# One chain for the head groups, the short convolution of blocks 2 and 3 inside the delta-rule groups, and w3's low parts on VectorE

## The chip, the cores and the metric

The kernel runs on one core of a Trainium2 chip. Its engines work at the same time and wait for each other by semaphores: TensorE (PE for matmuls, PEld for the weight loads beside them), VectorE (DVE), ScalarE (ACT), GpSimd (POOL) and SyncE (SP), which here issues every DMA. Each engine takes its own instructions in the order in which they stand in the program. The metric is device microseconds of one execution, lower is better: the median of some runs. A profile is one further execution, taken by the hardware profiler.

## What is computed

One layer of a streaming encoder for 2048 prompt tokens and 32 sample tokens with their own states, D = 1024. All heads read one normalised input through one projection; their outputs are joined by W_out, and a SwiGLU block and a gated input embedding follow:

```python
hn = rmsnorm(h, W['norm_mix'][i])
proj = hn @ W['w_in'][i]
qkv_pre, z, ba, u5, cc = jnp.split(proj, [OFF_Z, OFF_BA, OFF_S5, OFF_CC], axis=-1)
ya, s_gdn, b_gconv = gdn_mixer(qkv_pre, z, ba, ...)   # conv of width 4 + silu on q, k, v, then the delta rule
yb, s_s5 = s5_mixer(u5, ...)                          # 16 groups x 64 complex states, then gelu and a GLU
yc, b_conv = conformer_conv(cc, ...)                  # GLU, causal depthwise conv of width 31, LayerNorm, swish
h = h + jnp.concatenate([ya, yb, yc], axis=-1) @ W['w_out'][i]
hf = rmsnorm(h, W['norm_ffn'][i])
h = h + (jax.nn.silu(hf @ W['ffn_w1'][i]) * (hf @ W['ffn_w3'][i])) @ W['ffn_w2'][i]
h = h + (p[i] @ W['pe_w'][i]) * jax.nn.sigmoid(h @ W['pe_gate_w'][i])
y = rmsnorm(h, W['norm_final'])
```

The outputs are y, and the new states of the delta rule, of both convolutions and of S5, for prompt and sample. The delta rule carries its state from chunk to chunk, so its blocks run one after the other; S5 and the two convolutions need only the projections of their block and what a block hands to the next.

## The kernel before

**Tiling.** Features lie on partitions, tokens along the row. The tokens make four blocks of 512; the last one has the 32 sample tokens too (544, done as two halves of 272). Phase A runs over the blocks 0 to 3 (called A0 to A3 here) and makes the projections; phase F runs over the same blocks (F0 to F3): w_out, the hidden layer with w1 and w3, w2, then pe and gate, then the final norm.

**Dense matmuls.** An fp32 operand is split in a high and a low part, and each product is made of three passes: high weight by high input, low by high, high by low (`dense`, `_dense`, L120: 8 input tiles by 3 passes is a group of 24 matmuls). `load_weight` (L81 to L104) loads a weight by DMA (`wr`), ScalarE copies the high part (L94, `wh`), and the low part `wl` is subtracted by GpSimd the first time (L96), stored in DRAM (`lo_`), and loaded from there by the later blocks. So subtractions of phase F's weights happen in F0 alone. Weights have three buffers each; `dense` writes into three PSUM buffers (`ps_d`), which VectorE empties.

**Phase A** (`PhaseA.block`): for each block the squares and norm, `u5` (L657), the gate and value of the conformer's GLU (`ccg`, `cca`, L707 to L712, stored as `xcd`), then twelve short convolutions (`PhaseA.conv`: the projection goes to `raw`, L607, then one scaled copy and three fused multiply-adds into `gacc`, L612 to L614, tanh and one more step, L617, stored as `sild`), then four `z` (L730 to L733, stored as `zgd`).

**Heads.** Everything else of the mixers is in generators: `conf` (62 multiply-adds `cacc` on VectorE a block, L813, then transposes, statistics L827, `cxn` L846 to L851, stored to `mixT` at L852), `gdn_group` (half a block of 256 tokens, and one for the sample tokens; triangular solve, transpose `XT` L961, state `S`, `zy` L1079, stored to `mixT` at L1080), `s5_unit` (two blocks at once; `X` L498, `ps_y` L518, `gq` L537, `ps_glu` L547) and, once, `s5_init` (the S5 constants; `ps_kg` L352). `dense` calls `G.step`, and each time enough matmul columns have gone by, every running chain of generators emits its next piece and says with `yield k` for how many further steps it pauses. This sets the order in which the program is written; a scheduler then sets the order on each engine, by the ranks `first`, `heads` and `later` and by its own model of times.

**Order before.** After A0, `s5_init` is emitted whole, at rank `heads`. During A1 to A3 one chain runs conformer block 0 and delta-rule block 0, and from A2 a second one runs S5 unit 0. Both are flushed at the end of phase A. In F0 to F2 a chain runs the conformer and delta-rule block of the next block, in F0 S5 unit 1 behind them, and each chain is flushed at the end of its block:

```python
for b in range(NB):
    nb = b + 1
    if nb < NB:
        G.start(run(conf_of(nb), gdn_of(nb), *(s5_of(u) for u in range(1, G.NU) if max(u * G.UB - 2, 0) == b)))
    pf.block(b)
    G.flush()
```

**Queue.** `PhaseF.block` begins with loads of `mixT` into `hb` (L1124), which need all heads of its block, splits them in `fah` (ScalarE) and `fal` (L1105, VectorE or GpSimd) for w_out, and adds the input (L1126). It ends with the final norm (L1222) and eight stores `out_yT` (L1223). All of these DMAs stand in one queue, SP's, in the order of the program, with the loads of weights between them.

Of the kernel before, what the change touches and what calls it, by code (L numbers as in the profile page):

```python
# [8 lines left out]
F32 = mybir.dt.float32  # L9
# [7 lines left out]
P = 128  # L17
# [63 lines left out]
def load_weight(G, src, K, name, key):  # L81


    nc = G.nc
    shp = [P] + (list(K) if isinstance(K, tuple) else [K]) + [P]
    with G.first():
        wr = G.wraw.tile(shp, F32, tag="wr", name=f"wr_{name}")
        nc.sync.dma_start(wr, src)
        wh = G.whi.tile(shp, F32R, tag="wh", name=f"wh_{name}")
        wl = G.wlo.tile(shp, F32R, tag="wl", name=f"wl_{name}")  # L90
        kept = G.low.get((name, key))
        if kept is not None:
            nc.sync.dma_start(wl.bitcast(F32), kept)
        nc.scalar.activation(wh, wr, AF.Copy)  # L94
        if kept is None:
            nc.gpsimd.tensor_tensor(wl, wr, wh.bitcast(F32), op=ALU.subtract)  # L96
            if G.NB > 1:
                kept = G.dd.tile(shp, F32, tag=f"lo_{name}{key}", name=f"lo_{name}{key}")
                G.low[(name, key)] = kept
                nc.sync.dma_start(kept, wl.bitcast(F32))  # L100
    return wh, wl
# [105 lines left out]
def s5_init(G, A, tp, pspool):  # L207
# [78 lines left out]
    for m in (1, 2, 4):  # L286
# [128 lines left out]
def s5_unit(G, A, u, wp, pspool):  # L415
# [14 lines left out]
    for jq in range(4):  # L430
# [17 lines left out]

        yield 2

# [54 lines left out]

        yield 2

# [29 lines left out]
        V.scalar_tensor_tensor(gq[:, jh], t, 1.0, yf, op0=ALU.add, op1=ALU.mult)  # L537
        yield 2
    spc = 512 // NCT
# [23 lines left out]
class PhaseA:  # L563


    def __init__(self, G, A, ctx):
# [13 lines left out]
        self.gm = const("gmix", [P, KD], A.norm_mix)  # L580
        self.cw = const("cw", [P, 12, 4], A.conv_w)
        V.tensor_scalar(self.cw, self.cw, 0.5, None, op0=ALU.mult)
        wr = G.wraw.tile([P, KD, 8], F32, tag="wr", name="wr_ba")
# [8 lines left out]
    def conv(self, m, jj, b, hf, hl, bc, n, last, t0):  # L592
# [16 lines left out]
        if last:  # L609
            nc.gpsimd.tensor_copy(taild[:, m], raw[:, W:W + 3])  # L610
        acc = wp.tile([P, W], F32, tag="gacc", name="gacc")
        nc.scalar.activation(acc, raw[:, 0:W], AF.Copy, scale=cw[:, m, 0:1])  # L612
# [9 lines left out]
    def block(self, b):  # L622
# [76 lines left out]
        for j in range(2):  # L699
# [13 lines left out]
            if not last:  # L713
                nc.sync.dma_start(G.xcd[b + 1][:, j, 0:30], xc[:, BLK - 30:BLK])
        with G.later():
            for g in gs:
                for _ in g:
                    pass
        for h in range(NH):
            self.conv(4 + h, 2 * h, b, hf, hl_, bc, n, last, t0)  # L720
            self.conv(h, 2 * h + 1, b, hf, hl_, bc, n, last, t0)
        for h in range(NH):
            self.conv(8 + h, 8 + h, b, hf, hl_, bc, n, last, t0)
        for h in range(NH):
            w = load_weight(G, A.w_in[12 + h], KD, "z", h)
            zz = wp.tile([P, n], F32, tag="gacc", name="zz")
            for c0, cn in chunks_of(n):
                cs = slice(c0, c0 + cn)
                p_ = dense(G, G.psD, "pd", w, hf, hl_, ks, c0, cn)
                V.tensor_tensor(zz[:, cs], p_[:, :cn], bc[:, cs], op=ALU.mult)  # L730
            th = wp.tile([P, n], F32, tag="gth", name="zth", bufs=1)
            nc.scalar.activation(th, zz, AF.Tanh, scale=0.5)
            V.scalar_tensor_tensor(zz, th, 1.0, zz, op0=ALU.add, op1=ALU.mult)  # L733
            nc.sync.dma_start(G.zgd[b][:, h], zz)
# [120 lines left out]
def gdn_group(G, A, sp, pspool, T, tw, nt, nw, S, b, c_out):  # L855
# [8 lines left out]
    kq = sp.tile([P, 8, nn], F32, tag="kq", name="kq", bufs=1)  # L864
    nc.sync.dma_start(kq, G.sild[b][:, 0:8, c_out:c_out + nn])
    vf = sp.tile([P, NH, nn], F32, tag="vf", name="vf", bufs=1)
    nc.sync.dma_start(vf, G.sild[b][:, 8:12, c_out:c_out + nn])
    yield 2
# [92 lines left out]
    V.transpose(XT.rearrange("p w c -> p (w c)"), X.rearrange("p w c -> p (w c)"))  # L961
    yield 3

# [263 lines left out]
def trunk_kernel(ctx: ExitStack, tc: tile.TileContext, A):  # L1227
# [56 lines left out]
    G.mixT = [dd.tile([P, KD, n], F32, tag=f"mixT{b}", name=f"mixT{b}") for b, n in enumerate(G.ns)]  # L1284
    G.sild = [dd.tile([P, 12, n], F32, tag=f"sild{b}", name=f"sild{b}") for b, n in enumerate(G.ns)]
    G.zgd = [dd.tile([P, NH, n], F32, tag=f"zgd{b}", name=f"zgd{b}") for b, n in enumerate(G.ns)]
# [23 lines left out]
    with G.heads():  # L1310
# [55 lines left out]
    def run(*gens):  # L1366

        for g in gens:
            yield from g

    with ExitStack() as cx:
        pa = PhaseA(G, A, cx)
        pa.block(0)
        with R("s5i") as tp, G.heads():
            s5_init(G, A, tp, G.psM)

        with R("s5_0") as w5:
            G.start(run(conf_of(0), gdn_of(0)))
            for b in range(1, NB):
                if b == G.UB:  # L1380
                    G.start(s5_unit(G, A, 0, w5, G.psM))
                pa.block(b)
            if NB == G.UB:
                G.start(s5_unit(G, A, 0, w5, G.psM))
            G.flush()
    pf = PhaseF(G, A, ctx)
    for b in range(NB):
        nb = b + 1
        if nb < NB:

            G.start(run(conf_of(nb), gdn_of(nb), *(s5_of(u) for u in range(1, G.NU) if max(u * G.UB - 2, 0) == b)))
        pf.block(b)
        G.flush()

# [114 lines left out]
```

## Time and profile before

| what | value |
|---|---|
| median of three runs | 2914.17 us (2912.3 to 2915.87) |
| the profiled execution | 2906.6 us |
| its span in the trace | 2904.8 us |
| mean granted TensorE clock | 0.976 |
| busy: PE, DVE, ACT, POOL | 2775.6, 1769.2, 931.4, 625.4 us |
| stages, by the first matmul of each: A1, A2, A3 | 189.5, 336.8, 521.3 us |
| F0, F1, F2, F3 | 706.9, 1291.5, 1835.5, 2367.5 us |

The trace's span is 1.8 us shorter than its execution's time. The busy time of an engine counts its instructions from start to end; a busy PE at a clock under 1 does less. A row of the waits names the instruction that waited, `<-`, and the one that released it, then the total, how many times and the longest. A row of the timeline has a start, a duration, engine, line, operation, `out<-in`, shape and count; in brackets is the idle time before it.

### The profile page before, as it was taken

How to read it: one execution, taken by the hardware profiler on the slowest of the kernel's cores; microseconds unless marked ns; L12 is line 12 of the kernel's file. 1: busy time of each engine (PE TensorE's matmuls, PEld its weight loads, DVE VectorE, ACT ScalarE, POOL GpSimd, SP SyncE). 2: the span in 40 equal slices, each digit the busy share in tenths (PEclk: the TensorE clock that was granted, in tenths of full speed). 3: DMA queues.
4: the chain of work that ended last, by engine and by line, in shares of the span. 5: the costliest groups of instructions: out<-in, count | busy, mean ns of one | idle time of the engine just before them, and what ended most of it. 6: DMA issues, size and time to landing. Idle time of an engine off the chain costs nothing.

```text
span 2904.8 us, 40874 instructions
## 1 busy us (share of the span) xinstructions
PE 2775.6 (96%) x15300; PEld 2373.5 (82%) x15300; DVE 1769.2 (61%) x3812; ACT 931.4 (32%) x1382; POOL 625.4 (22%) x482
## 2 busy tenths in 40 slices
PE   7789999899999999898999999999999999999997
PEld 5668777798878778676888887888888789999997
DVE  8989768896675856676663645954454543333343
ACT  4244433334322222233322323432222343222232
POOL 5733222133543434441010100110000010000000
PEclk9989999999999999899999999999999999999998
DMA  6577776657654546565565656765565574555553
GB/s 217 186 261 245 234 206 222 190 169 242 218 176 161 187 152 225 172 205 204 190 199 160 208 167 222 243 203 179 186 190 167 178 269 158 175 174 175 175 188 104
DMA packets 280566, 565.16 MB, mean 195 GB/s; under 512 B 68993, under 2 KB 128529, under 8 KB 280225
## 3 DMA queue, kind: packets, MB, share of 16 engines
q1 hardware_dynamic: 280368, 562.55, 60.1%
q8 instruction: 121, 1.98, 0.3%
q14 instruction: 77, 0.62, 0.1%
HBM read 457.67 MB, written 104.20 MB: 193 GB/s over the span
## 4 chain that ended last, share of the span: by engine, by line
PE 73%; DVE 14%; DMA 8%; issue 2%; SPq 2%; ACT 1%; POOL 0%; DVEq 0%; ACTq 0%; POOLq 0%
PE ps_d L120 65%; DVE gacc L614 1%; DVE cx L952 1%; DMA sild<-gacc 1%; DMA cu<-ud 1%; DVE ct L951 1%; PE ps_q L982 1%; DMA xk<-in_xT 1%; DMA mixT<-zy 1%; PE ps_z L995 1%; DVE cacc L813 1%; PE ps_kk L904 1%; DMA zy<-zgd 1%; DVE X L498 1%; PE ps_ks L1025 1%
## 5 line engine op out<-in xcount | busy, mean ns | idle before, releaser
L94 ACT ACTIVATE wh_w<-wr_w 128x1024 fp32r<-128x1024 f32 (+1 forms) x272 | 281.3, 1034 | 841.3 <-PE ps_d L120 596.5
L120 PE MATMUL ps_d<-fah,wh_w 128*128 128x512 f32 (+1 forms) x1760 | 382.0, 355 | 7.8 <-DVE hb L1142 3.4
L120 PE MATMUL ps_d<-fal,wh_w 128*128 128x512 f32 (+1 forms) x1760 | 379.2, 354 | 0.0
L120 PE MATMUL ps_d<-fah,wl_w 128*128 128x512 f32 (+1 forms) x1760 | 375.5, 352 | 0.0
L120 PEld LDWEIGHTS ps_d<-fah,wh_w 128*128 128x128 f32 x1760 | 290.7, 189 | 52.4 <-issue 4.9
L120 PEld LDWEIGHTS ps_d<-fal,wh_w 128*128 128x128 f32 x1760 | 291.4, 189 | 42.7
L120 PEld LDWEIGHTS ps_d<-fah,wl_w 128*128 128x128 f32 x1760 | 290.8, 188 | 42.8
L1187 DVE TENSOR_TENSOR hb<-hb,ps_d 128x512 f32<-128x512 f32 (+1 forms) x240 | 140.1, 585 | 181.7 <-PE ps_d L120 180.7
L120 PE MATMUL ps_d<-acth,wh_w 128*128 128x512 f32 (+1 forms) x880 | 208.3, 355 | 8.0 <-DVE hb L1187 4.5
L96 POOL TENSOR_TENSOR wl_w<-wr_w,wh_w 128x1024 fp32r<-128x1024 f32 (+1 forms) x68 | 160.7, 2365 | 237.3 <-ACT wh_w L94 229.5
L120 PE MATMUL ps_d<-acth,wl_w 128*128 128x512 f32 (+1 forms) x880 | 209.4, 354 | 0.0
L120 PE MATMUL ps_d<-actl,wh_w 128*128 128x512 f32 (+1 forms) x880 | 209.1, 355 | 0.0
L813 DVE SCALAR_TENSOR_TENSOR cacc<-xc,cc_w,cacc 128x512 f32<-128x512 f32 (+1 forms) x240 | 178.8, 779 | 0.0
L120 PEld LDWEIGHTS ps_d<-acth,wh_w 128*128 128x128 f32 x880 | 148.8, 189 | 34.3 <-DVE hb L1187 6.9
L120 PEld LDWEIGHTS ps_d<-actl,wh_w 128*128 128x128 f32 x880 | 150.1, 190 | 22.4
L120 PEld LDWEIGHTS ps_d<-acth,wl_w 128*128 128x128 f32 x880 | 149.8, 189 | 22.3
L1170 DVE SCALAR_TENSOR_TENSOR fth<-ps_d,bc 128x512 f32<-128x512 f32 (+1 forms) x110 | 64.8, 589 | 135.4 <-PE ps_d L120 134.8
L1165 DVE TENSOR_TENSOR fa<-ps_d,bc 128x512 f32<-128x512 f32 (+1 forms) x110 | 64.7, 589 | 128.8 <-PE ps_d L120 115.5
L1168 DVE SCALAR_TENSOR_TENSOR fa<-fth,fa 128x512 f32<-128x512 f32 (+1 forms) x110 | 92.3, 839 | 73.4 <-ACT fth L1167 73.2
L614 DVE SCALAR_TENSOR_TENSOR gacc<-raw,cw,gacc 128x512 f32<-128x512 f32 (+1 forms) x144 | 118.9, 828 | 27.4 <-ACT gacc L612 24.8
L1173 DVE TENSOR_TENSOR actl<-fa,acth 128x512 fp32r<-128x512 f32 (+1 forms) x110 | 85.5, 778 | 48.6 <-ACT acth L1172 48.4
L120 PE MATMUL ps_d<-hh,wl_qkv 128*128 128x512 f32 (+1 forms) x480 | 108.2, 362 | 5.9 <-POOL wl_qkv L96 5.9
(468 smaller groups left out, 4817.1 us busy)
## 6 DMA issues: line engine op xcount, KB each, us to landing
wr_w<-in_w SPq DMA_DIRECT2D x256, 512.0 KB, 4.0
wl_w<-lo_w SPq DMA_DIRECT2D x192, 512.0 KB, 3.5
lo_w<-wl_w SPq DMA_DIRECT2D x64, 512.0 KB, 3.0
wr_qkv<-in_w_in SPq DMA_DIRECT2D x48, 512.0 KB, 4.0
wl_qkv<-lo_qkv SPq DMA_DIRECT2D x36, 512.0 KB, 4.3
wr_out<-in_w_out SPq DMA_DIRECT2D x32, 512.0 KB, 4.9
wr_gate<-in_pe_gate SPq DMA_DIRECT2D x32, 512.0 KB, 4.6
sild<-gacc SPq DMA_DIRECT2D x48, 256.0 KB, 4.1
```

Of the source, the lines that this page charges most:

```text
L94: nc.scalar.activation(wh, wr, AF.Copy)
L96: nc.gpsimd.tensor_tensor(wl, wr, wh.bitcast(F32), op=ALU.subtract)
L120: nc.tensor.matmul(ps[:, :cn], a[:, i, :], x(k)[:, c0:c0 + cn], start=start and p_ == 0 and i == 0, stop=stop and p_ == 2 and i == K - 1)
L498: V.tensor_tensor(X[h][half[i], :, 1:], a[half[h], :, :NC], b_[half[h], :, :NC], op=op)
L614: V.scalar_tensor_tensor(acc, raw[:, t:t + W], cw[:, m, t:t + 1], acc, op0=ALU.mult, op1=ALU.add)
L813: V.scalar_tensor_tensor(acc[:, j], xc[:, j, t:t + W], cn_.w[:, j, t:t + 1], acc[:, j], op0=ALU.mult, op1=ALU.add)
L904: nc.tensor.matmul(kk4[:, h - h0], kq[:, 2 * h, cw], kq[:, 2 * h:2 * h + 2, cw], start=True, stop=True)
L1165: V.tensor_tensor(a, p1[:, :cn], bc[:, cs], op=ALU.mult)
L1168: V.scalar_tensor_tensor(a, th, 1.0, a, op0=ALU.add, op1=ALU.mult)
L1170: V.scalar_tensor_tensor(th, p3[:, :cn], 0.5, bc[:, cs], op0=ALU.mult, op1=ALU.mult)
L1173: V.tensor_tensor(fb[:, cs], a, fa[:, cs].bitcast(F32), op=ALU.subtract)
L1187: V.tensor_tensor(hb[m][:, c0:c0 + cn], hb[m][:, c0:c0 + cn], p_[:, :cn], op=ALU.add)
```

## The change

Four things are changed, and they are independent in the code.

1. `load_weight`: the low part of w3 is subtracted by VectorE, all others as before by GpSimd. 22 weights of 128x1024 are meant, all in F0.
2. `G.raw = {2, 3}`: for blocks 2 and 3 `PhaseA.conv` stores the raw projection with its halo of three columns, and `gdn_group` loads it, with three more columns, into the buffers of AQ, X and XT and makes the copies, the multiply-adds, tanh and the last step itself, in 128x256 pieces, with pauses between.
3. `s5_init` becomes a generator at the head of the first chain, followed by delta-rule block 0 and then conformer block 0. S5 unit 0 has its own chain from A2 on, as before, and begins when `s5_init` is done. The flush at the end of phase A stays. For phase F there is one chain over the blocks 1 to 3 (conformer, in block 2 S5 unit 1, delta rule), started ahead of F0; ahead of `pf.block(b)` it is flushed only as far as block b's heads, and no longer behind each block.
4. Pauses: `s5_unit` 2 to 3, 2 to 4, and 2 to 1 or 5; behind the XT transpose of `gdn_group` 3 to 5. In `PhaseA.block` the second half of `gates` is emitted behind the convolutions. `conv_w`'s constant moves to `G.cw`.

```diff
@@ load_weight
-            nc.gpsimd.tensor_tensor(wl, wr, wh.bitcast(F32), op=ALU.subtract)
+            e = nc.vector if name == "w3" else nc.gpsimd
+            e.tensor_tensor(wl, wr, wh.bitcast(F32), op=ALU.subtract)
@@ s5_unit
-        yield 2
+        yield 3
...
-        yield 2
+        yield 4
...
-        yield 2
+        yield 1 if jh == 0 else 5
@@ PhaseA.conv
+        if b in G.raw:
+            nc.sync.dma_start(G.sild[b][:, jj], raw)
+            return
@@ gdn_group
+    if b in G.raw:
+        c0 = c_out + (3 if c_out >= BLK else 0)
+        raws = [sp.tile([P, 4, nn + 3], F32, tag=tg, name="raw" + tg, bufs=1) for tg in ("AQ", "X", "XT")]
+        for i in range(3):
+            nc.sync.dma_start(raws[i], G.sild[b][:, 4 * i:4 * i + 4, c0:c0 + nn + 3])
+        yield 2
+        for i, dst in enumerate((kq[:, 0:4], kq[:, 4:8], vf)):
+            for x in range(4):
+                m = 8 + x if i == 2 else (2 * i + x // 2) + (4 if x % 2 == 0 else 0)
+                a = dst[:, x]
+                nc.scalar.activation(a, raws[i][:, x, 0:nn], AF.Copy, scale=G.cw[:, m, 0:1])
+                for t in range(1, 4):
+                    V.scalar_tensor_tensor(a, raws[i][:, x, t:t + nn], G.cw[:, m, t:t + 1], a, op0=ALU.mult, op1=ALU.add)
+            th = sp.tile([P, 4, nn], F32, tag="U", name="cth", bufs=1)
+            nc.scalar.activation(th, dst, AF.Tanh)
+            V.scalar_tensor_tensor(dst, th, 1.0, dst, op0=ALU.add, op1=ALU.mult)
+            yield 2
...
-    yield 3
+    yield 5
@@ trunk_kernel
-    def flush():
-        while G.chains:
+    def flush(done=lambda: False):
+        while G.chains and not done():
             G.chains = [c for c in G.chains if advance(c)]
...
+        def first_s5():
+            while "w5" not in box:
+                yield 1
+            yield from s5_unit(G, A, 0, box["w5"], G.psM)
+            box["done"] = True
+
+        def first_heads():
+            with R("s5i") as tp:
+                yield from s5_init(G, A, tp, G.psM)
+            with R("s5_0") as w5:
+                box["w5"] = w5
+                yield from gdn_of(0)
+                yield from conf_of(0)
+                while "done" not in box:
+                    yield 1
...
+    ready = [0]
+
+    def later_heads():
+        for b in range(1, NB):
+            yield from conf_of(b)
+            if b % G.UB == 0:
+                yield from s5_of(b // G.UB)
+            yield from gdn_of(b)
+            ready[0] = b
+
+    G.start(later_heads())
     for b in range(NB):
-        nb = b + 1
-        if nb < NB:
-
-            G.start(run(conf_of(nb), gdn_of(nb), *(s5_of(u) for u in range(1, G.NU) if max(u * G.UB - 2, 0) == b)))
+        G.flush(lambda: ready[0] >= b)
         pf.block(b)
-        G.flush()
```

How this moves instructions is shown at three places. The lines of the changed kernel have other numbers: L730 and L733 (`zz`) became L741 and L744, L813 (`cacc`) L824, L851 (`cxn`) L862, L1105 (`fal`) L1134, L120 L122.

**From A3 to F0.** VectorE before, from the last steps of A3's `zz` to the first of F0's `fal`:

```order
L733 SCALAR_TENSOR_TENSOR zz<-zth,zz 128x544
L730 TENSOR_TENSOR zz<-ps_d,bc 128x272 x2
L1105 TENSOR_TENSOR fal<-hb,fah 128x512 x5
L733 SCALAR_TENSOR_TENSOR zz<-zth,zz 128x544
L851 SCALAR_TENSOR_TENSOR cxn<-cth,cxn 128x512
```

VectorE after, from the last steps of A3's `zz` to the statistics of conformer block 0 (`cst`, `cmv`); the first `fal` of F0 stands 29 rows behind the 46:

```order
L741 TENSOR_TENSOR zz<-ps_d,bc 128x272
L824 SCALAR_TENSOR_TENSOR cacc<-xc,cc_w,cacc 128x512 x5
L744 SCALAR_TENSOR_TENSOR zz<-zth,zz 128x544
L824 SCALAR_TENSOR_TENSOR cacc<-xc,cc_w,cacc 128x512 x46
L838 BN_STATS cst<-ctk 128x6
L839 BN_AGGR cmv<-cst 128x2
```

The same place on SP, after; `mixT_59` is block 0's, `mixT_60` block 1's:

```order
L1128 DMA g_6863<-in_norm_final 128x8
L863 DMA mixT_59<-cxn 128x512 x2
L1153 DMA hb<-mixT_59 128x512 x7
L1155 DMA hb<-in_xT 128x512
L1153 DMA hb<-mixT_59 128x512
```

Before, conformer block 0 lies in A1 and its two stores to `mixT_59` stand some 240 rows of SP ahead of F0's loads.

**From F2 to F3.** PE after, from the last gate group of F2 (its last pass) into the sample tokens' delta-rule group (`ps_vn`, `ps_s`, `ps_o`) and the final norm (`ps_ss`):

```order
L122 MATMUL ps_d<-fal,wh_gate 128x512 x8
L1067 MATMUL ps_vn<-rk,X 32x128 x4
L151 MATMUL ps_ss<-ones,ssum_20034 128x1 x4
L1074 MATMUL ps_s<-vn,rk 128x128 x4
L1081 MATMUL ps_o<-Sd_19706,kq 32x128
```

After three more such pairs of `ps_o` it ends with these and goes on with F3's w_out (272 wide):

```order
L1082 MATMUL ps_o<-vn,AQ 32x128
L134 MATMUL ps_bc<-ident,rso 128x128 x4
L1107 MATMUL ps_ot<-ident,o 128x32 x4
L122 MATMUL ps_d<-fah,wh_out 128x272 x22
L122 MATMUL ps_d<-fah,wl_out 128x272 x8
```

Before, the last gate pass is followed by `L120 MATMUL ps_d<-fah,wh_out 128x272 x8` directly, and the sample group lies ahead of it, among F2's last w2, pe and gate groups. SP after, from the sample group's `X` (L989) to the loads of F3 (`mixT_62`); the eight `out_yT` are F2's result:

```order
L989 DMA X<-xd 32x4x32
L88 DMA wr_out<-in_w_out 128x1024
L1103 DMA zy<-zgd_70 128x4x32
L1381 DMA out_gdn_s<-S 128x512
L1252 DMA out_yT<-hb 128x512 x8
L1109 DMA mixT_62<-zy 128x4x32
L1153 DMA hb<-mixT_62 128x544 x8
```

**From F0 to F1.** PE before, the end of S5 unit 1 (`ps_y`, then `ps_glu` among F1's first w_out groups):

```order
L518 MATMUL ps_y<-XD_11335,c_G 128x4
L120 MATMUL ps_d<-fal,wh_gate 128x512 x5
L120 MATMUL ps_d<-fah,wh_out 128x512 x8
L120 MATMUL ps_d<-fah,wl_out 128x512 x6
L547 MATMUL ps_glu<-gq,glu 128x396 x2
```

PE after, the same steps, now among the groups of w2 in F1:

```order
L527 MATMUL ps_y<-XD_12206,c_G 128x4
L122 MATMUL ps_d<-actl,wh_w_12710 128x512 x4
L122 MATMUL ps_d<-acth,wh_w_12756 128x512 x4
L122 MATMUL ps_d<-acth,wl_w_12757 128x512
L556 MATMUL ps_glu<-gq,glu 128x396
```

The unit as a whole went from the second half of F0 into F1, and conformer block 2, which stood in F1, to F0's end.

More of the change, by code (lines that the diff above doesn't have):

```diff
@@ L327, in s5_init @@
         cmul(nc, tmp, C.Hre[:, :, l], C.nHim[:, :, l], cre0, cim0, bc(Lre[:, l]), bc(Lim[:, l]))
+        if l % 3 == 2:
+            yield 1
     V.tensor_scalar(C.nHim, C.nHim, -1.0, None, op0=ALU.mult)
@@ L361, in s5_init @@
         nc.sync.dma_start(C.Toep[l * 16:(l + 1) * 16, :, (7 - l) * 16:P].rearrange("p g (l c) -> p g l c", c=16), kg[:, :, 0:l + 1])
+    yield 1
     NC = G.UB * BLK // L5
@@ L381, in s5_init @@
         m *= 2
+        yield 1
     a = big[0][:, :, :NC]
@@ L580, in __init__ @@
         self.gm = const("gmix", [P, KD], A.norm_mix)
-        self.cw = const("cw", [P, 12, 4], A.conv_w)
-        V.tensor_scalar(self.cw, self.cw, 0.5, None, op0=ALU.mult)
+        self.cw = G.cw
         wr = G.wraw.tile([P, KD, 8], F32, tag="wr", name="wr_ba")
@@ L714, in block @@
                 nc.sync.dma_start(G.xcd[b + 1][:, j, 0:30], xc[:, BLK - 30:BLK])
[L715 to L718, printed above, removed]
         for h in range(NH):
@@ L723, in block @@
             self.conv(8 + h, 8 + h, b, hf, hl_, bc, n, last, t0)
+        with G.later():
+            for g in gs:
+                for _ in g:
+                    pass
         for h in range(NH):
@@ L864, in gdn_group @@
     kq = sp.tile([P, 8, nn], F32, tag="kq", name="kq", bufs=1)
-    nc.sync.dma_start(kq, G.sild[b][:, 0:8, c_out:c_out + nn])
     vf = sp.tile([P, NH, nn], F32, tag="vf", name="vf", bufs=1)
-    nc.sync.dma_start(vf, G.sild[b][:, 8:12, c_out:c_out + nn])
+    if b in G.raw:
[14 more added lines that the diff above has]
+            V.scalar_tensor_tensor(dst, th, 1.0, dst, op0=ALU.add, op1=ALU.mult)
+            yield 2
+    else:
+        nc.sync.dma_start(kq, G.sild[b][:, 0:8, c_out:c_out + nn])
+        nc.sync.dma_start(vf, G.sild[b][:, 8:12, c_out:c_out + nn])
     yield 2
@@ L1284, in trunk_kernel @@
     G.mixT = [dd.tile([P, KD, n], F32, tag=f"mixT{b}", name=f"mixT{b}") for b, n in enumerate(G.ns)]
-    G.sild = [dd.tile([P, 12, n], F32, tag=f"sild{b}", name=f"sild{b}") for b, n in enumerate(G.ns)]
+    G.raw = set(range(2, NB))
+    wid = lambda b: G.ns[b] + (3 + 3 * (b == NB - 1) if b in G.raw else 0)
+    G.sild = [dd.tile([P, 12, wid(b)], F32, tag=f"sild{b}", name=f"sild{b}") for b in range(NB)]
     G.zgd = [dd.tile([P, NH, n], F32, tag=f"zgd{b}", name=f"zgd{b}") for b, n in enumerate(G.ns)]
@@ L1315, in trunk_kernel @@
         G.strict = const("strict", [P, P], A.c_strict)
+        G.cw = const("cw", [P, 12, 4], A.conv_w, half=True)
         G.mhalf = cp.tile([P, 1], F32, tag="mhalf", name="mhalf")
@@ L1373, in trunk_kernel @@
         pa.block(0)
[L1374 to L1384, printed above, removed]
-            G.flush()
-    pf = PhaseF(G, A, ctx)
+        box = {}
+        def first_s5():
+            while "w5" not in box:
+                yield 1
+            yield from s5_unit(G, A, 0, box["w5"], G.psM)
[8 more added lines that the diff above has]
+                while "done" not in box:
+                    yield 1
+        G.start(first_heads())
+        for b in range(1, NB):
+            if b == G.UB:
+                G.start(first_s5())
+            pa.block(b)
+        if NB == G.UB:
+            G.start(first_s5())
+        G.flush()
+    pf = PhaseF(G, A, ctx)
+    ready = [0]
+    def later_heads():
+        for b in range(1, NB):
+            yield from conf_of(b)
[4 more added lines that the diff above has]
+    G.start(later_heads())
     for b in range(NB):
-        nb = b + 1
-        if nb < NB:
-            G.start(run(conf_of(nb), gdn_of(nb), *(s5_of(u) for u in range(1, G.NU) if max(u * G.UB - 2, 0) == b)))
+        G.flush(lambda: ready[0] >= b)
         pf.block(b)
-        G.flush()
 def _layout(np, d):
```

## Prediction

> **What bounds the kernel now.** The page's first part, its row of granted clocks, then the trace cut at the eight stages (phase A over blocks 0 to 3, phase F over blocks 0, 1 and 3; columns: stretch, length, busy us of PE, PEld, DVE, ACT, POOL, clock, DMA share, GB/s):
>
> ```profile
> PE 2775.6 (96%) x15300; PEld 2373.5 (82%) x15300; DVE 1769.2 (61%) x3812; ACT 931.4 (32%) x1382; POOL 625.4 (22%) x482
> ...
> PEclk9989999999999999899999999999999999999998
> ...
> 0.00:189.50 189.50, 154.81 (x644) 118.75 (x644) 166.47 (x403) 66.64 (x100) 114.06 (x110) 0.92 0.66 219
> 189.50:336.80 147.30, 140.33 (x628) 111.80 (x629) 126.41 (x258) 61.99 (x93) 43.43 (x43) 0.97 0.76 244
> 336.80:521.30 184.50, 174.73 (x914) 140.75 (x912) 142.87 (x350) 68.13 (x109) 51.40 (x59) 0.96 0.70 216
> 521.30:706.90 185.60, 171.04 (x1311) 162.24 (x1310) 148.51 (x390) 64.90 (x112) 44.38 (x61) 0.97 0.59 189
> 706.90:1291.50 584.60, 557.25 (x2658) 458.30 (x2657) 388.37 (x675) 170.06 (x242) 256.58 (x125) 0.96 0.57 188
> 1291.50:1835.50 544.00, 530.32 (x2513) 434.13 (x2513) 311.62 (x646) 174.40 (x250) 45.56 (x33) 0.99 0.61 195
> ```
>
> TensorE bounds it. What can be won is its idle time and the clock it lost: length less PE, plus busy time times one less the clock. That gives 34.7 + 12.4 = 47 us in A0, 11 in A1, 17 in A2, 20 in A3 (95 in phase A: 66 idle, 29 clock), 27 + 22 = 50 in F0 and 14 + 5 = 19 in F1. In A0 VectorE is busier than PE. The waits of PE (total, times, longest) say who is late:
>
> ```profile
> PE ps_y L518 <- DVE X L498: 13.7, 3, 5.5
> PE ps_d L120 <- DVE zz L730: 13.4, 4, 4.9
> PE ps_d L657 <- ACT hh L77: 10.6, 6, 6.4
> PE ps_glu L547 <- DVE gq L537: 8.7, 2, 6.4
> PE ps_d L120 <- POOL wl_qkv L96: 5.9, 1, 5.9
> ...
> PE ps_gc L780 <- issue: 5.1, 1, 5.1
> PE ps_q L982 <- DVE XT L961: 4.7, 2, 3.5
> PE ps_kg L352 <- ACT kg L354: 4.4, 1, 4.4
> ...
> PE ps_q L982 <- DVE g_p L771: 4.2, 1, 4.2
> ...
> PE ps_d L120 <- DVE hb L1142: 3.4, 1, 3.4
> ...
> PE ps_d L120 <- DVE raw L607: 2.4, 3, 1.6
> ...
> PE ps_d L120 <- DVE fa L1165: 2.3, 2, 2.1
> ```
>
> **The change, part by part.** Sums go against the profiled execution (2906.6 us, span 2904.8), which is 7.6 under the median.
>
> *Phase A, less.* Conformer block 0 (62 accumulations) leaves A1, the short convolution of blocks 2 and 3 leaves A2 and A3, and s5_init is spread over stages. I let go the waits of phase A that are behind this VectorE work: zz 13.4, ps_gc 5.1, kg 4.4, g_p 4.2, raw 2.4, the smaller glu wait 2.3, and 2.1 of hh: 34 of 66 us. The start, wl_qkv and the first norm stay, because the first eleven matmul groups of A0 keep the same VectorE and GpSimd work. Of the clock's 29 us I let the same share go, 15. **−49**; bounds −20 (the waits return under the other heads) and −65.
>
> *Short convolution inside the groups.* Each block's 36 steps, about 30 us of this row, now run as 128x256 pieces in F1 and F2:
>
> ```profile
> L614 DVE SCALAR_TENSOR_TENSOR gacc<-raw,cw,gacc 128x512 f32<-128x512 f32 (+1 forms) x144 | 118.9, 828 | 27.4 <-ACT gacc L612 24.8
> ```
>
> In F1 VectorE has 544 − 312 = 232 us free, which covers it; without that cover it would cost 30 a block. But group 2 now ends only about 12 us ahead of F1's end: **+3** there (0 to 8). The extra load per group is one DMA issue, on a queue that waits elsewhere: 0.
>
> *w3's low parts on VectorE.* 22 GpSimd steps go; VectorE gets 22, each about twice the second row (twice the width), 1.35 us, so 30 us:
>
> ```profile
> L96 POOL TENSOR_TENSOR wl_w<-wr_w,wh_w 128x1024 fp32r<-128x1024 f32 (+1 forms) x68 | 160.7, 2365 | 237.3 <-ACT wh_w L94 229.5
> ...
> 2298.01 0.68 DVE L1105 TENSOR_TENSOR fal<-hb,fah 128x512 fp32r<-128x512 f32 x1
> ```
>
> No wait of PE above is for wl_w, so the GpSimd time is worth nothing by itself; three weight buffers and three PSUM buffers hide VectorE's 30, F0 having 196 free: **0**, bounds −20 and +30. Against the zero speaks a second cost of GpSimd's work, told by small VectorE steps in A0 beside it and without it:
>
> ```profile
> 32.65 2.35 DVE L68 TENSOR_TENSOR rst<-rsy 128x4 f32<-128x4 f32 x1
> ...
> 265.48 0.16 DVE L68 TENSOR_TENSOR rst<-rsy 128x4 f32<-128x4 f32 x1
> ```
>
> The same step took fifteen times as long, though it has 16 bytes a partition. [...]
>
> *F0, less.* S5 unit 1 moves from F0 to F1, with longer pauses. Its ps_y waits (13.7) go, also XT's 4.7 by the longer pause behind the transpose. The half-clock stretches lie around them:
>
> ```profile
> 1161.90:1234.50 72.60, 60.50 (x270) 49.76 (x270) 45.05 (x91) 18.49 (x28) 32.31 (x20) 0.84 0.57 172
> ...
> 1248.00:1268.00 20.00, 16.54 (x66) 14.53 (x67) 12.39 (x30) 5.63 (x9) 4.71 (x2) 0.74 0.57 186
> ```
>
> Lost there: 0.16 × 60.5 + 0.26 × 16.5 = 14. Conformer block 2 takes the place at F0's end, for which I give back 5 (its like costs 5.5 in F1 now: hb 3.4, fa 2.1). **−27**, bounds −35 and −10.
>
> *F1, less; F2, more.* glu 6.4, hb 3.4, fa 2.1 and 3 of the clock go, and unit 1 brings 3: **−12**. Conformer block 3 starts F2: **+6**.
>
> *A3 to F0, a new hole.* After the change VectorE's row has 46 accumulations of conformer block 0 behind the last zz and ahead of the first fal of F0, and SP holds both stores of cxn ahead of the first load of hb. So nothing of F0 can start, and PE has nothing else.
>
> ```profile
> 1374.12 4.06 DVE L813 SCALAR_TENSOR_TENSOR cacc<-xc,cc_w,cacc 128x512 f32<-128x512 f32 x6
> ...
> 1413.13 0.74 DVE L813 SCALAR_TENSOR_TENSOR cacc<-xc,cc_w,cacc 128x512 f32<-128x512 f32 x1
> ...
> 1444.15 0.69 DVE L851 SCALAR_TENSOR_TENSOR cxn<-cth,cxn 128x512 f32<-128x512 f32 x1 [1.73 <-ACT cth L850]
> ...
> hb<-mixT SPq DMA_DIRECT2D x24, 256.0 KB, 6.7
> ...
> mixT<-cxn SPq DMA_DIRECT2D x6, 256.0 KB, 2.9
> ```
>
> One step is (4.06 − 0.75) / 5 = 0.66 us, so 46 are 30.5. From the last one to the second cxn a block takes 31 us in F1, with dense groups of PE between its steps; alone I take half, 15 (10 to 28). Store 2.9, load 6.7, zz and split 1.1. That is 56, and 3 for the clock, less than the 4.7 a wait that the ps_y waits cost (14 over three): **+59**, 51 to 72.
>
> *F2 to F3, a second hole.* The sample group now ends behind F2's last gate matmul: ps_vn to ps_ot stand there in PE's row, and SP holds eight out_yT stores and mixT<-zy ahead of hb. Those stores wait for block 2's final norm, which VectorE does ahead of zy. The end of F3 shows that norm uncovered; the other rows are the sample group's tail and its transfers:
>
> ```profile
> 2882.34 1.18 PE L120 MATMUL ps_d<-fal,wh_gate 128*128 128x272 f32 x8
> ...
> 2893.58 6.88 DVE L1222 SCALAR_TENSOR_TENSOR hb<-hb,g,bc 128x544 f32<-128x544 f32 x5 [2.66 <-ACT bc L137]
> ...
> 2307.64 0.70 DVE L1065 SCALAR_TENSOR_TENSOR oms<-oms,or 32x4 f32<-32x4 f32 x1
> ...
> 2318.23 0.35 DVE L1079 SCALAR_TENSOR_TENSOR zy<-ps_ot,gnw,zy 128x128 f32<-128x128 f32 x1 [4.00 <-PE ps_ot L1078]
> ...
> mixT<-zy SPq DMA_DIRECT2D x16, 256.0 KB, 3.5
> ...
> hb<-mixT SPq DMA_DIRECT2D x8, 272.0 KB, 4.6
> ```
>
> From the gate's end (2883.5) to the norm's last step (2900.5) are 17 us. From the group's own norm to zy it took 10.9, mostly behind dense groups; alone half, 5. Store 3.5, load 4.6, split 0.7: 31, with the clock **+34** (23 to 42).
>
> [...]
>
> **Sum.** −49 − 27 − 12 + 0 + 59 + 34 + 3 + 6 = +14: span 2919, run 2921, on the median's basis **2928 us**. A chip tells about 0.2% (6 us) from no change.
>
> **Rivals.**
> [...]
> *Slower by more: the tails are as long as beside dense work.* The first hole 72, the second 42, phase A only 35: −74 + 123 = +49, **2963**. For it: SP is one queue, and loads of weights stand in it. Against: the long tails of today contain matmuls that the holes don't have.
> *w3's subtraction comes late.* VectorE runs in order; each of the 22 holds an evacuation 1.35 us and its own weights; were none hidden, +30, **2958**. Against: three buffers, and no wait for wl_w today.
> *The change doesn't do what its order says*: block 0 done before A3's end, no first hole: −59, **2869**. Against: VectorE is in order, and the 46 stand behind the last zz.
>
> **Chances.** Forecast 0.5 (own range 2908 to 2948), faster rival 0.25, slower 0.14, w3 0.06, no hole 0.05. Faster by over 0.2%: 0.05 + 0.23 + 0.02 of the forecast's = 0.30. Within: 0.02 + 0.13 = 0.15. Slower: 0.35 + 0.14 + 0.06 = 0.55. The range, 2880 to 2966, takes in all but the no-hole case and the outer ends.
>
> **What the profile after would show.** One stretch of 50 to 72 us between A3's last z matmul and F0's first w_out matmul with PE empty and VectorE in cacc, then a wait for hb's load; another of 23 to 42 between F2's last gate matmul and the first 272-wide w_out matmul, ended by hb's load behind out_yT; no ps_y wait over 2 us at F0's end; A0 at about 165 to 175 us in place of 189.5, A2 and A3 shorter by some 10 each. If the first hole is under 45 us, or phase A is over 50 us shorter ahead of it, my sign is wrong. If F0 holds waits of PE for wl_w, w3's price was wrong.

## The result and the profile after

The changed kernel took 2946.95 us (median of 4 runs, 2946.29 to 2947.25) against 2913.78 us before in the same runs: a ratio of 1.0113, 95% interval 1.0095 to 1.0131, slower by 33 us. The forecast was 2928, slower by 14: the sign and the range held, the size was under half. The profiled execution has a span of 2945.4 us, 40.6 longer than the one before; that one had run 7 us below its kernel's median.

Of the page after, the row of granted clocks; then the trace cut at the first w_out or wba matmul of each stage, with the two holes as stretches of their own (A0 to A3, the hole, F0, F1, F2, the second hole, F3; columns as in the prediction):

```profile
PEclk9899999995999999999999999999999979999998
...
0.00:185.50 185.50, 151.61 (x626) 116.59 (x627) 166.91 (x398) 66.09 (x98) 107.10 (x109) 0.93 0.65 218
185.50:323.70 138.20, 137.71 (x632) 109.79 (x631) 93.46 (x229) 59.72 (x86) 25.21 (x38) 1.00 0.83 262
323.70:494.60 170.90, 165.54 (x877) 134.56 (x876) 94.95 (x274) 52.91 (x85) 39.03 (x53) 0.99 0.75 227
494.60:674.90 180.30, 171.54 (x1335) 162.99 (x1333) 118.81 (x320) 46.11 (x80) 35.71 (x62) 0.97 0.61 191
674.90:734.80 59.90, 9.53 (x34) 4.86 (x33) 47.48 (x88) 7.95 (x15) 9.44 (x11) 0.52 0.17 58
734.80:1286.10 551.30, 530.04 (x2479) 431.32 (x2478) 382.21 (x622) 169.96 (x243) 188.55 (x89) 0.98 0.55 185
1286.10:1835.70 549.60, 544.02 (x2690) 448.45 (x2688) 312.80 (x759) 188.92 (x275) 59.37 (x46) 1.00 0.65 201
1835.70:2374.10 538.40, 529.32 (x2528) 433.06 (x2528) 340.93 (x813) 188.52 (x288) 46.48 (x36) 0.99 0.61 194
2374.10:2405.90 31.80, 11.88 (x48) 7.41 (x48) 13.54 (x27) 4.09 (x7) 6.60 (x5) 0.55 0.38 129
2405.90:2945.40 539.50, 518.24 (x4062) 514.93 (x4062) 193.16 (x410) 154.64 (x235) 17.05 (x12) 0.97 0.51 168
```

The 5 and the 7 in the clock's row are the two holes. By the prediction's own measure, idle time plus lost clock, the stages give (F2 and F3 before: 1 and 32 us lost):

| | forecast | measured |
|---|---|---|
| A0 to A3 | −49 | 66 lost in place of 95: −29 |
| hole ahead of F0 | +59 | 50.4 idle, 4.6 of lost clock: +55 |
| F0 | −27 | 32 in place of 50: −18 |
| F1, with the start of F2 | −12 + 3 | 6 in place of 19: −13 |
| F2 | +6 | 14 in place of 1: +13 |
| hole ahead of F3 | +34 | 19.9 idle, 5.3 of lost clock: +25 |
| F3 | 0 | 37 in place of 32: +5 |
| sum | +14 | +38 (the span: +40.6; the clocks are rounded) |

The waits of PE after. The first and the fourth lie in the holes; those for raw (2.4 us before; now all four lie in A0) and for hb of w2 (5.5 us before; now most of it in the second half of F0) have grown:

```profile
PE ps_ct L835 <- DVE cacc L824: 39.0, 1, 39.0
PE ps_d L122 <- DVE hb L1216: 17.0, 12, 2.9
PE ps_d L122 <- DVE raw L615: 14.3, 4, 6.1
PE ps_ot L1107 <- DVE o L1099: 10.1, 1, 10.1
PE ps_d L122 <- ACT fah L1132: 9.3, 2, 5.7
```

The timeline of PE, VectorE and SP through the hole ahead of F0:

```profile
673.30 1.62 PE L122 MATMUL ps_d<-hl,wh_z 128*128 128x272 f32 x8
...
683.95 30.55 DVE L824 SCALAR_TENSOR_TENSOR cacc<-xc,cc_w,cacc 128x512 f32<-128x512 f32 x46
...
725.62 4.80 SPq L863 DMA_DIRECT2D mixT<-cxn  x2
...
729.40 0.67 DVE L862 SCALAR_TENSOR_TENSOR cxn<-cth,cxn 128x512 f32<-128x512 f32 x1
...
730.48 3.67 SPq L1153 DMA_DIRECT2D hb<-mixT  x7
...
734.76 7.42 PE L122 MATMUL ps_d<-fah,wh_out 128*128 128x512 f32 x22
```

The steps are those forecast, in their order. The 46 accumulations took 30.6 us (30.5 forecast), and 15.6 passed from the last of them to the second cxn (15 forecast). But the 46 began 9.0 us behind A3's last z matmul, and only 4.7 us passed from the second cxn to the first matmul of F0, where the forecast had 10.7 for store, load, zz and split. The granted clock stands at 0.50 from 678 to 738 us, at 0.71 in the two us from there, and at 1.00 from 740 on. The 22 matmuls then take 7.4 us in place of 22 × 0.23 = 5.1 (0.23 is their spacing from 749.85 us on, eight in 1.84): at this hole the clock's price behind it is 2.3, not my 3.

The hole ahead of F3, the same way:

```profile
2371.64 2.00 PE L122 MATMUL ps_d<-fal,wh_gate 128*128 128x512 f32 x8
2378.24 1.91 PE L1067 MATMUL ps_vn<-rk,X 32*32 32x128 f32 x8 [4.60 <-DMA X<-xd]
...
2390.36 6.38 DVE L1251 SCALAR_TENSOR_TENSOR hb<-hb,g,bc 128x512 f32<-128x512 f32 x5
...
2400.63 0.38 SPq L1109 DMA_DIRECT2D mixT<-zy  x1
2402.48 3.69 SPq L1153 DMA_DIRECT2D hb<-mixT  x8
...
2405.95 1.38 PE L122 MATMUL ps_d<-fah,wh_out 128*128 128x272 f32 x4 [5.73 <-ACT fah L1132]
```

From the gate's end to the last step of the final norm it took 23 us (17 forecast), from there to zy 4 (5), and on to the first matmul 5 (9): 32 in place of 31. PE is busy with the sample group in 12 us of it.

### The profile page after: what moved, and what is told of

It reads as the page before. It is cut to its first block, busy times and chain, and to the rows that moved or that the text cites. A ratio compares the mean times of both kernels' runs of the same rounds, so it can differ in the third digit from the quotient of the medians.

```text
span 2945.4 us, 40970 instructions
## 1 busy us (share of the span) xinstructions
PE 2769.4 (94%) x15300; PEld 2364.0 (80%) x15300; DVE 1764.2 (60%) x3933; ACT 938.9 (32%) x1409; POOL 534.5 (18%) x460
## 4 chain that ended last, share of the span: by engine, by line
PE 69%; DVE 14%; DMA 8%; issue 5%; ACT 1%; SPq 1%; POOL 1%; DVEq 0%; ACTq 0%; POOLq 0%
PE ps_d L122 60%; DVE cacc L824 4%; DMA xk<-in_xT 1%; DVE cx L981 1%; DMA mixT<-zy 1%; DVE gacc L625 1%; PE ps_kk L933 1%; DVE ct L980 1%; PE ps_q L1011 1%; PE ps_z L1024 1%; DMA cu<-ud 1%; PE ps_o L1081 1%; PE ps_o L1082 1%; PE ps_vn L1067 1%; DVE hb L1216 1%
## 5 line engine op out<-in xcount | busy, mean ns | idle before, releaser
L122 PE MATMUL ps_d<-fah,wh_w 128*128 128x512 f32 (+1 forms) x1760 | 378.1, 354 | 6.7 <-DVE fa L1194 3.0
L122 PE MATMUL ps_d<-fal,wh_w 128*128 128x512 f32 (+1 forms) x1760 | 379.3, 354 | 0.0
L122 PE MATMUL ps_d<-fah,wl_w 128*128 128x512 f32 (+1 forms) x1760 | 377.8, 353 | 0.0
L122 PEld LDWEIGHTS ps_d<-fah,wh_w 128*128 128x128 f32 x1760 | 291.2, 189 | 51.9 <-DVE fa L1194 3.4
L122 PEld LDWEIGHTS ps_d<-fal,wh_w 128*128 128x128 f32 x1760 | 291.9, 189 | 43.7 <-issue 0.5
L122 PEld LDWEIGHTS ps_d<-fah,wl_w 128*128 128x128 f32 x1760 | 291.4, 189 | 42.7
L122 PE MATMUL ps_d<-acth,wh_w 128*128 128x512 f32 (+1 forms) x880 | 209.6, 355 | 17.8 <-DVE hb L1216 13.7
L122 PE MATMUL ps_d<-acth,wl_w 128*128 128x512 f32 (+1 forms) x880 | 209.7, 354 | 0.0
L122 PE MATMUL ps_d<-actl,wh_w 128*128 128x512 f32 (+1 forms) x880 | 207.5, 353 | 0.0
L824 DVE SCALAR_TENSOR_TENSOR cacc<-xc,cc_w,cacc 128x512 f32<-128x512 f32 (+1 forms) x240 | 194.4, 858 | 0.0
L122 PEld LDWEIGHTS ps_d<-acth,wh_w 128*128 128x128 f32 x880 | 147.7, 189 | 46.0 <-DVE hb L1216 12.9
L122 PEld LDWEIGHTS ps_d<-acth,wl_w 128*128 128x128 f32 x880 | 149.1, 189 | 22.4
L122 PEld LDWEIGHTS ps_d<-actl,wh_w 128*128 128x128 f32 x880 | 149.1, 188 | 22.3
L98 POOL TENSOR_TENSOR wl_w<-wr_w,wh_w 128x1024 fp32r<-128x1024 f32 (+1 forms) x46 | 111.3, 2421 | 269.4 <-ACT wh_w L94 238.5
L122 PE MATMUL ps_d<-hh,wh_qkv 128*128 128x512 f32 (+1 forms) x480 | 109.1, 368 | 13.8 <-DVE raw L615 13.7
L1197 DVE SCALAR_TENSOR_TENSOR fa<-fth,fa 128x512 f32<-128x512 f32 (+1 forms) x110 | 74.0, 674 | 58.7 <-ACT fth L1196 58.6
L122 PE MATMUL ps_d<-hh,wl_qkv 128*128 128x512 f32 (+1 forms) x480 | 105.5, 361 | 2.6 <-POOL wl_qkv L98 2.1
L1201 ACT ACTIVATE acth<-fa 128x512 fp32r<-128x512 f32 (+1 forms) x110 | 60.3, 548 | 143.0 <-DVE fa L1200 142.8
```

Of the source, the lines that this page charges most:

```text
L98: e.tensor_tensor(wl, wr, wh.bitcast(F32), op=ALU.subtract)
L122: nc.tensor.matmul(ps[:, :cn], a[:, i, :], x(k)[:, c0:c0 + cn], start=start and p_ == 0 and i == 0, stop=stop and p_ == 2 and i == K - 1)
L824: V.scalar_tensor_tensor(acc[:, j], xc[:, j, t:t + W], cn_.w[:, j, t:t + 1], acc[:, j], op0=ALU.mult, op1=ALU.add)
L1197: V.scalar_tensor_tensor(a, th, 1.0, a, op0=ALU.add, op1=ALU.mult)
L1201: nc.scalar.activation(fa[:, cs], a, AF.Copy)
```

## The experiments

The kernel before took 2907.41, 2906.71 and 2907.35 us in the three sets of runs; by its ratio the changed kernel would be at 2940 there. Stage lengths are from each kernel's trace.

**e1, heads of phase A as before.** The first chain is again `run(conf_of(0), gdn_of(0))`, `s5_init` runs at once behind A0.

> The changed kernel with the heads of phase A as they were before it (s5_init at once behind A0, chain of conformer block 0 then delta-rule block 0, S5 unit 0 from A2); all else as changed. My theory, the hole of 60 us ahead of F0 comes from conformer block 0 standing behind delta-rule block 0: the hole is gone, and VectorE in A0 and A1 is as before, so A1 gives its 9 us back: 2947 - 56 + 9 = about 2900 us. Rival, the hole comes from VectorE being overfull at the end of A3 (conformer block 1 is pulled in there too): 25 us or more of a hole stay, 2920 us or more. In both the hole of 32 us ahead of F3 stays, because it is made in F1 and F2.

2903.86 us, ratio 0.9985 (0.9976 to 0.9994), as the theory said. PE goes on without a gap from A3 to F0:

```profile
694.86 1.16 PE L122 MATMUL ps_d<-hl,wh_z 128*128 128x272 f32 x8
695.86 0.60 PE L835 MATMUL ps_ct<-ident,cacc 128*128 128x128 f32 x4
696.21 3.72 PE L122 MATMUL ps_d<-fah,wh_out 128*128 128x512 f32 x15
```

A0 to A3 last 696 us in place of 675 and a hole of 60. So the new order of phase A's heads made the phase 21 us shorter, and paid 60 for it. The hole ahead of F3 stays, with 32 us, as expected.

**e10, conformer block 0 first**, the order of the chain alone:

```diff
-                yield from gdn_of(0)
                 yield from conf_of(0)
+                yield from gdn_of(0)
```

> The changed kernel with conformer block 0 ahead of delta-rule block 0 in the first chain, nothing else. The 46 accumulations then don't stand behind A3; the last steps of delta-rule block 0 (ps_s to ps_ot) and conformer block 1's transposes do, by the order on PE. By the theory that whatever ends the first chain is uncovered: a hole of 15 to 30 us in place of 60, 2905 to 2920 us on the basis of 2947. By the theory that the accumulations alone made it: none, 2890 us.

2908.28 us, ratio 0.9999 (0.9990 to 1.0008). The hole is 27 us, and delta-rule block 0 ends in it, beside the statistics and stores of conformer block 1. So what ends the chain is uncovered here too; how long the hole is depends on the piece.

**e2, no convolution in the groups**: `G.raw = set()`.

> The changed kernel with the short convolution of blocks 2 and 3 back in phase A. Theory, the hole ahead of F3 is the groups of F1 and F2 getting longer one behind the other (their raw projections share the buffers AQ, X and XT, so a group's convolution can't begin before the group ahead of it is done): without it the hole of 32 us goes, and F2 loses 10 us less; A2 and A3 take back 17 us of VectorE's work: 2947 - 26 - 10 + 17 = about 2928 us. Rival, one chain that isn't flushed and its longer pauses make that hole: it stays, and the time is 2947 + 17 = 2964 us.

2927.96 us, ratio 1.0079 (1.0061 to 1.0097), as the theory said. The hole ahead of F3 is gone:

```profile
2384.47 2.00 PE L122 MATMUL ps_d<-fal,wh_gate 128*128 128x512 f32 x8
2386.31 1.13 PE L122 MATMUL ps_d<-fah,wh_out 128*128 128x272 f32 x7
```

F2 is 5 us shorter, A3 23 longer (203 us), A2 the same.

**e6, the convolution alone**, on the kernel before. The second half of `gates` stays behind the convolutions here, as in the change, so the edit is not quite the convolution alone.

> The kernel before with nothing changed but the short convolution of blocks 2 and 3 in the delta-rule groups; chains, flushes and pauses as before. Theory, the hole ahead of F3 is the convolution's alone: it is there with about 32 us (26 lost), F2 loses 10 more, A2 and A3 together give 20: about 16 us over the kernel before of the same runs. Rival, it takes the one chain as well: no hole, A2 and A3 give 20, so 20 us under it.

2917.08 us, ratio 1.0037 (1.0024 to 1.0050). The hole is there with 27 us, F2 is 9 longer, and A3 14 shorter. So neither the one chain nor the pauses are needed for it, and the later gates alone don't make it, since e2 has them and no hole. The convolution moves work that makes A3 14 to 23 us longer into a chain of groups that then ends behind F2.

**e4, w3 back on GpSimd**, all else as changed.

> The changed kernel with w3's low parts back on GpSimd. By the prediction (nothing waits for them, VectorE's 30 us are hidden) no change, 2947 us within 4. By theory A (blocked VectorE) F0 becomes longer, by up to 22 x 2.2 = 48 us of VectorE, of which I expect 10 to 20 to reach PE: about 2960 us. By theory B (VectorE overfull) F0 becomes shorter by 5 to 15: about 2937 us.

2953.06 us, ratio 1.0153 (1.0138 to 1.0168): F0 562.5 us in place of 551.3. A move that I had priced at nothing was worth 11 us in the changed kernel.

**e5, w3 alone**, on the kernel before.

> The kernel before with nothing changed but w3's low parts on VectorE. Theory A (GpSimd's subtractions block VectorE all over F0): F0 gives about the 11 us that e4 lost, so 11 us under the kernel before of the same runs. Rival (w3's move pays only where conformer block 2 lies in F0, which it doesn't here): within 3 us of the kernel before.

2881.16 us, ratio 0.9909 (0.9893 to 0.9926): 26 us, more than theory A asked for. F0 takes 565 us in place of 584, F1 4 less.

**e3, all low parts on VectorE**: `e = nc.vector`.

> The changed kernel with every weight's low part subtracted by VectorE, not w3's alone. It tells two theories of why A0 and F0 won so little. A, VectorE is blocked by GpSimd's subtractions (14 of conformer block 2's 60 accumulations in F0 took over 1 us, 18.7 us too much): none of them takes over 1 us any more, and A0 and F0 become shorter by 10 to 20 us each, about 2925 us. B, VectorE simply has too much work there: A0 gets 22 more steps of 1.35 us, F0 46, and they become longer, by up to 30 and 60 us, 2975 us or more. Both holes stay.

2942.54 us, ratio 1.0119 (1.0104 to 1.0134), no change as a whole, and neither theory's total. By stages: F0 is 526.6 us in place of 551.3, as theory A said (3 of the 60 accumulations still took over 1 us). A0 got no shorter: its last z matmul ends at 185 us in both, and the first wba matmul of A1 comes at 190.7 in place of 185.5, though VectorE is busy 147 us there in place of 167. PE waits 28 us for raw and zz in it, in place of 14; what made these late stays open. Later stages gave the gain back: F1 557 in place of 546, 14 us ahead of F2 in place of 4, F2 4 longer. Conformer block 2's accumulations end at 1243 us here, at 1245 in the changed kernel: the heads seem to keep their own pace in us; F0 ended 28 us earlier, and what they had not done by then would be left to F1 and to the gap ahead of F2. That is argued from these times, not tested.

**e7, w2, pe and gate on VectorE as well as w3.**

> The changed kernel with the low parts of w2, pe and gate on VectorE too (w_out's and w1's stay on GpSimd, phase A's too). If conformer block 2 at the end of F0 meeting these GpSimd steps is what ate F0's gain: at most 3 of its accumulations take over 1 us in place of 14, F0 falls from 551 us to 527 to 535, as with all of them moved. If w_out's and w1's steps were as much to blame, F0 stays at 540 or more. Both holes stay, the one ahead of F2 grows from 4 to about 14 us.

2943.12 us, ratio 1.0124 (1.0109 to 1.0139). F0 is 528.5 us, so it is the second half's GpSimd steps that matter. The whole gains nothing: the gap ahead of F2 is 14 us, as in e3. The accumulations of conformer block 2 before (in F1), after and in e7 (both in F0; durations in ns: least, median, most):

```profile
L813 DVE SCALAR_TENSOR_TENSOR cacc<-xc,cc_w,cacc x60: 741/746/752, 1353.4 to 1413.1; 128x512 f32<-128x512 f32 x60
```

```profile
L824 DVE SCALAR_TENSOR_TENSOR cacc<-xc,cc_w,cacc x60: 735/739/2894, 1162.1 to 1244.5; 128x512 f32<-128x512 f32 x60
```

```profile
L824 DVE SCALAR_TENSOR_TENSOR cacc<-xc,cc_w,cacc x60: 736/744/1187, 1163.8 to 1245.0; 128x512 f32<-128x512 f32 x60
```

After, 14 of the 60 took over 1 us, some 19 us too much in all, each while GpSimd was at a subtraction; in e7 two did. Two of them as they stand in the changed kernel, VectorE and GpSimd at the same moment:

```profile
1187.19 3.99 DVE L824 SCALAR_TENSOR_TENSOR cacc<-xc,cc_w,cacc 128x512 f32<-128x512 f32 x2
...
1185.09 5.54 POOL L98 TENSOR_TENSOR wl_w<-wr_w,wh_w 128x1024 fp32r<-128x1024 f32 x2 [5.95 <-ACT wh_w L94]
```

Two accumulations take 1.4 us elsewhere; these take 4.0 and end at 1191.2, half a us after GpSimd's two subtractions (1190.6).

**e9, s5_init behind A0**, on the kernel before: one added step makes it wait for the last z of A0.

> The kernel before, with S5's constants (s5_init) made to wait for the last z of A0 by one added step (zero times a piece of zz, added to log_dt). It asks what A0's lost 46 us are; only A0's length counts here, since the heads behind it come late and will leave a hole ahead of F0. If s5_init's steps on VectorE and GpSimd hold A0 up: A0 falls from 189.5 us to 160 to 172. If it is the convolution and GpSimd's subtractions of A0's own weights: 180 or more.

It was run once. A0 and A1:

```profile
0.00:151.20 151.20, 134.27 (x565) 104.24 (x566) 113.63 (x168) 62.14 (x90) 70.98 (x61) 0.99 0.64 218
151.20:315.70 164.50, 145.00 (x646) 113.44 (x645) 138.65 (x397) 59.16 (x87) 49.65 (x81) 0.93 0.75 250
```

A0 is 38 us shorter, more than asked for, and VectorE's time in it 114 us in place of 166. Its lost time fell from 47 us to 18; the other 9 are work that went with s5_init, 79 matmuls fewer. A1 takes 17 of the 38 back. Ahead of F0 the late heads leave a hole of 68 us (2954 us in all), so it is no way to win by itself.

**e11, all low parts of phase F on VectorE**, nothing else, on the kernel before.

> The kernel before with all low parts of phase F's weights on VectorE, not w3's alone, nothing else. By theory A (blocked VectorE) F0 falls further than the 565 us of w3 alone, to 540 to 550, and the whole is 35 to 45 us under the kernel before of the same runs. If VectorE's 40 further steps eat it: as w3 alone, 26 us under, or less.

2860.32 us, ratio 0.9834 (0.9818 to 0.9851), 47 us under the kernel before and the best of all. Its F0, below the kernel before's, then one group of VectorE's steps in F0 before and in e11, and a second group whose steps read one operand from PSUM:

```profile
707.40:1291.80 584.40, 557.05 (x2655) 458.02 (x2654) 388.17 (x675) 169.86 (x241) 256.08 (x125) 0.96 0.57 188
```

```profile
713.50:1251.40 537.90, 533.70 (x2607) 441.00 (x2605) 358.83 (x729) 172.19 (x244) 51.83 (x37) 0.99 0.60 201
...
L97 DVE TENSOR_TENSOR wl_w<-wr_w,wh_w x68: 685/1225/2064, 748.1 to 1173.2; 128x1024 fp32r<-128x1024 f32 x64, 128x512 fp32r<-128x512 f32 x4
```

```profile
L1168 DVE SCALAR_TENSOR_TENSOR fa<-fth,fa 128x512 f32<-128x512 f32 x22 | 41.5, 1888 | 15.5 <-ACT fth L1167 15.5
L1187 DVE TENSOR_TENSOR hb<-hb,ps_d 128x512 f32<-128x512 f32 x48 | 32.7, 684 | 29.2 <-PE ps_d L120 28.9
```

```profile
L1169 DVE SCALAR_TENSOR_TENSOR fa<-fth,fa 128x512 f32<-128x512 f32 x22 | 15.6, 708 | 0.2
L1188 DVE TENSOR_TENSOR hb<-hb,ps_d 128x512 f32<-128x512 f32 x48 | 32.8, 686 | 23.2 <-PE ps_d L121 22.7
```

VectorE has 84 subtractions more there, some 100 us at 1.2 us each, and is busy 29 us less; 30 of its other steps went to other stages. Over the whole kernel, where nothing but the 86 subtractions (107 us) came, it is busy 1752.1 us in place of 1769.2. PE's waits in F0 fell from 27 us (for X, XT, hb and ct) to 4.

**e8 and e12, combinations.** e8: heads of phase A as before, no convolution in the groups, the one chain, the pauses and the order of gates as changed, low parts of phase F on VectorE. e12: e11 with the change's pauses and its order of gates, so e8 without the one chain.

> A combination: heads of phase A as before the change (no hole ahead of F0), no convolution in the groups (no hole ahead of F3), the one chain with its pauses in phase F, and all low parts of phase F's weights on VectorE. If the stages add up as measured one by one (F0 begins at 708, F0 527, F1 546, F2 533, F3 526 us, 12 behind it): 2852 us, some 55 us under the kernel before of the same runs. If VectorE's 46 further steps cost in F0 what the blocking cost, since without the earlier hole F0's first half is fuller: F0 545 or more, 2870 us or more.

> As the one with all low parts of phase F on VectorE, with the change's longer pauses and its later second half of gates as well; heads of both phases, flushes and convolution as before the change. The pauses take the 7 us of ps_y waits left in F0, gates 5 us of A1: some 10 us under the former, 45 to 55 under the kernel before.

2878.55 us (0.9905, 0.9891 to 0.9920) and 2889.01 us (0.9933, 0.9919 to 0.9948). Both are slower than e11, and both forecasts of them missed; e8's time lies where its rival put it, but its F0 (534 us) does not. In e8 A3 takes 199 us, 14 over the kernel before, and F2 541. In e12 A3 takes 197, F0 552 and F2 541 against 188, 538 and 533 in e11, and A1 142 against 148. So pauses and gates together cost about 29 us there; which of the two was not tried. The one chain of phase F seems to give 10 of it back (e8 against e12, whose intervals just touch).

## Why the prediction was right in sign and wrong in size

- **The hole ahead of F0, +59: right, +55, in part by luck.** 60 us with the steps named, ended by hb's loads; e1 takes it away. The accumulations and the tail to the second cxn came within 1 us. That the 46 begin 9 us behind the last z matmul I had not counted, and store and loads were 6 us shorter than I took them: two errors against each other.
- **The hole ahead of F3, +34: right in place and length, 9 too dear.** It is 32 us long, but I had counted all of it as lost, and PE does the sample group's matmuls in it. e2 and e6 show that the convolution in the groups makes it. I had named the place from the order, not the cause.
- **Phase A, −49: wrong, −29.** This is the largest miss, and it lies in A0: A0 took 185.5 us where I asked for 165 to 175, while A1 to A3 fell by 9, 14 and 5 us where I asked for some 10 each. The step that failed is letting the waits of A0 go because s5_init "is spread over stages". In the changed kernel most of its work on VectorE still runs in A0, at the same moment as before; one group of its steps before and after (start of the first and of the last):

```profile
L169 DVE TENSOR_TENSOR big<-cim,Lim x9: 279/280/283, 52.5 to 79.2; 128x128 f32<-128x128 f32 x9
```

```profile
L171 DVE TENSOR_TENSOR big<-cim,Lim x9: 275/277/283, 52.3 to 79.7; 128x128 f32<-128x128 f32 x9
```

VectorE is busy 166.9 us in A0 as against 166.5 before, and four waits for raw (14.3 us) stand in the place of those for ps_gc, kg and zz (12.2 there). e9 shows A0's loss to hang on s5_init. That A0's first eleven groups kept their work I had read from the order; that the rest kept theirs I had not.
- **F0, −27: wrong, −18, with two errors against each other.** w3, priced at **0**, gave 11 (e4), 19 of F0 alone on the kernel before (e5). So the rest of F0 gave 7 and not 27. The waits for ps_y and XT went as forecast (18.4 us, 1.5 left; beside them the granted clock had been 0.50 from 1166 to 1176, 1208 to 1220 and 1252 to 1260 us), but those for hb of w2 rose from 4.5 to 15.0: conformer block 2, for which I gave back 5, came to lie beside GpSimd's subtractions of w2, pe and gate. I had taken its price from F1, where GpSimd has none of them. e7 shows what they cost: these steps moved, F0 falls by 23. It is not conformer block 2 alone that suffers from them: in the kernel before, without that block in F0, moving all low parts but w3's took 27 us off F0 (e5 to e11).
- **w3.** My argument was that no wait of PE names wl_w. None does in any trace of this case, so the sign that I had set for a wrong price never showed, though the price was wrong. VectorE's steps took longer beside GpSimd's subtractions (one of 0.7 us took 2.9), and PE then waited for hb, X, XT or ct. By what mechanism they are held up, no run shows. My bound of −20 for w3 was an estimate that no run shows either, and I had not used it; e5 shows −26, and e11 −47 for all low parts of phase F.
- **F1, −9: −13, and S5 unit 1's own matmuls**, some 15 us, went there with it, which the measure by lost time leaves out. **F2, +6: +13**, of which the convolution makes 5 (e2) to 9 (e6); I had put its price into F1, at 3. F3's +5 stays unexplained.
- **The rivals.** The faster rival, to which I gave 0.25, asked for larger gains in phase A, F0 and F1 than the forecast's 85 us; the changed kernel has 60 there. "Slower by more", with 2963, came as near as the forecast, by its small gain in phase A (35, measured 29); the longer tails that it rested on were not there. Of "w3's subtraction comes late" nothing was seen.

What stays open: whether s5_init could run in A1 without a hole ahead of F0, and which of pauses and gates costs e12 its 29 us. I had counted the pauses as a gain (XT's 4.7, of which 3 went) and the gates as nothing. Measured one at a time, and with the gates in two of the terms, the parts of the change are: w3 −26 (e5), the convolution +10 (e6), the heads of phase A +36 (e1, against 2940), pauses and gates +29 (e12 against e11), the one chain −10 (e8 against e12). They add up to +39 for a change that measured +33; such a sum leaves out what the parts do to each other.

## What to carry to other kernels

Ask of each engine off the critical path not only who waits for its result, but whose steps take longer while it runs: here 86 steps of GpSimd that PE never waited for went with some 120 us more in VectorE's own steps (e11: 107 us of work came to it, and its busy time fell by 17). When heads, chains or pauses are moved, look at the end of each stage for what the last piece of a chain leaves uncovered, and at the stage's busy time for whether the work has really left it. A price read in one stage need not hold in another, where the other engines do something else.

## What was not expected of the hardware

VectorE with 86 more subtractions was busy 17 us less (e11), since its own steps took less time with GpSimd's gone: 22 steps of fa in F0 took 15.6 us in place of 41.5. The 48 steps of hb, which read one operand from PSUM, kept their length (32.7 and 32.8 us). The same subtraction took 1.2 us on VectorE and 2.4 us on GpSimd (medians of the changed kernel, 1225 and 2408 ns). Busy time of VectorE in the trace holds such longer steps, so 61% busy overstated its work.
